# The xbc projection's column tiles emitted one by one between the parts of two other mixers

## The chip, the cores and the metric

The kernel runs on one core of one Trainium2 chip (trn2). The metric is the device time of one execution in microseconds (us); the median over several runs counts. TensorE multiplies matrices into PSUM, ScalarE (ACT) copies PSUM results out and evaluates functions, VectorE (DVE) does elementwise work and scans, GpSimd (POOL) a little elementwise work, and SyncE (SP) issues the DMA transfers between HBM and SBUF.

## The reference, cut to what matters

Two network blocks follow each other on a sequence of 1024 tokens with 1024 features. The second begins with one projection whose columns feed three independent mixers:

```python
proj = h @ w_in                       # 1024 x 1024 tokens by features, times 1024 x 2312
z, xbc, dt_raw, u_s5, x_rg, g_rg = split(proj)   # 512, 1024, 8, 256, 256, 256 columns
xbc = silu(causal_dwconv(xbc, conv_w, conv_b))   # feeds the ssd mixer (8 chunks of 128 tokens)
y_s5 = s5_mixer(u_s5, ...)            # complex linear scan, gelu, a 256 x 256 gate
y_rg = rglru_mixer(x_rg, g_rg, ...)   # conv, two gates, linear scan, times gelu(g_rg)
y = concat([ssd_mixer(z, xbc, dt_raw), y_s5, y_rg]) @ w_out
h = layer_norm(ALPHA * h + y)         # then attention and an MLP
```

The xbc columns are needed only by the ssd mixer. The s5 and rg mixers do not read them.

## The kernel before, in words

The program is written as Python that emits instructions in order. At build time a scheduler fixes the order of each engine's queue: of the instructions whose inputs and buffers it expects to be there, it takes the one that was emitted first, so work emitted later can fill a hole if nothing it needs is missing. On the chip each queue runs strictly in that fixed order. SBUF buffers come from tagged pools with a fixed count of 4 KB-per-partition pages (line 51 and after): 8 of tag X, 8 of W, 8 of H, 6 of S, 3 of bc. Projections write into two PSUM buffers of tag mm.

Activations stand in SBUF as a pair of tiles, high and low part (tag U). A weight column block is loaded by `wcols` (line 100): 256 columns are two pages of 512 KB that are loaded into S (L91), cast to a high part in W by ACT (L82), and the low part is formed in W by DVE (L83); so a block of 256 columns takes 4 of the 8 W pages and, while it is loaded, 2 S pages. `feat_out` (line 367) then multiplies one 128-column tile by one half of the tokens with `mm3`: 8 slices times three matmuls (L114, L115, L116), 24 matmuls into one mm buffer.

The order of emission after the first block is `dt_proj`, `s5_mixer`, `xbc_proj`, `rg_mixer`, `ssd_setup`, the load of the output weights (`wout_load`, L659), then the eight ssd blocks woven with the output stage.

- `s5_mixer` (L1548 and after): a projection of 256 columns, transposes, 64 small matmuls (L1584), a chain on DVE of multiplications, two scans (L1598) and a complex product (L1360 to L1365), then for two halves m: 48 small matmuls each (L1625, L1628), a DVE addition (L1638), transposes (L1644), copies out by ACT (L1646, L1647), a gelu; and last a 256 x 256 gate (L1661 to L1667). It uses ten X pages: two each for UT, U, the scans Are and Aim, and H (eight at once), then one x for each half m.
- `xbc_proj` (L1179): four blocks c of 256 columns, two tiles each, j = 0 to 7. A tile is two `feat_out` calls, for each two ACT instructions that read the PSUM buffer (L1193 into `raw`, L1194 into `o`), then three DVE instructions (L1176), a tanh (L1197), a product (L1198) and the store to the DRAM tensor s_xbc (L1199). `raw` and `o` are X pages.
- `rg_mixer` (L1291): a projection of 256 columns with a conv, the load of the gate columns (Wg), 16 gate matmuls with Sigmoid and Tanh on ACT (L1329 to L1334), functions Ln, Exp and Sqrt on ACT (L1338 to L1343), scans on DVE (L1345), then the projection with Wg whose result is copied to X pages (L1351, L1352), gelu, product, store.
- `ssd_block(i)` loads a slice of all eight xbc tiles (L1213), so it waits for the last tile's store. It takes an S page at L1233 and feeds TensorE at L1243 to L1258.

Of the kernel before, what the change touches and what calls it, by code (L numbers as in the profile page):

```python
# [14 lines left out]
S = 1024  # L15
# [348 lines left out]
class Mix1(Net):  # L364
# [305 lines left out]
    def out_stage(self, W, srcs, res, finish):  # L670

        nc = self.nc
        for i in range(NB):
# [5 lines left out]
            if i == 0:  # L679
                P = self.page_pair()  # L680
            M = [P[z][:, :, 128 * i:128 * i + 128] if i < 4 else
                 self.page("H", F32R).rearrange("p (k c) -> p k c", c=128) for z in range(2)]
            self.split(st, M[0], M[1])
            y = self.page("H")
            nc.sync.dma_start(out=y, in_=_rows(res, i))
            for n in range(2):
                c = slice(512 * n, 512 * n + 512)
                ps = self.ps()
                self.mm3(ps, [(M[0][:, j, :], M[1][:, j, :]) for j in range(8)], W[n])
                self.add_res(y[:, c], ps, True)  # L690
# [371 lines left out]
class Mix2(Mix1):  # L1062


    def kv_mem(self):
        nc, I = self.nc, self.I
        M = [tuple(self.page("X", F32R, [128, 4, 256]) for _ in range(2)) for _ in range(2)]
        for t in range(2):
# [110 lines left out]
    def xbc_proj(self, T):  # L1179
        nc, I = self.nc, self.I  # L1180
        hw = self.small([128, 40], tag="hw", bufs=1)
        nc.vector.tensor_scalar(out=hw[:, 0:32], in0=self.pvec("ssd_conv_w"), scalar1=0.5, scalar2=None, op0=ALU.mult)
        nc.vector.tensor_scalar(out=hw[:, 32:40], in0=self.pvec("ssd_conv_b"), scalar1=0.5, scalar2=None, op0=ALU.mult)
        self.s_xd = self.dram([128, 8, S], "s_xbc")
        for c in range(4):
            W = self.wcols(I["w_in_2"], 512 + 256 * c, 256)
            for m in range(2):
                j = 2 * c + m
                raw, o = self.page("X"), self.page("X")
                for h in range(2):  # L1190
                    sl = slice(512 * h, 512 * h + 512)
                    ps = self.feat_out(T, W, slice(128 * m, 128 * m + 128), h)
                    nc.scalar.copy(out=raw[:, sl], in_=ps)  # L1193
                    nc.scalar.activation(out=o[:, sl], in_=ps, func=ACTF.Identity, scale=hw[:, 4 * j + 3:4 * j + 4],  # L1194
                                         bias=hw[:, 32 + j:33 + j])
                self.conv(o, raw, hw[:, 4 * j:4 * j + 4])
                nc.scalar.activation(out=raw, in_=o, func=ACTF.Tanh)  # L1197
                nc.vector.scalar_tensor_tensor(out=o, in0=raw, scalar=1.0, in1=o, op0=ALU.add, op1=ALU.mult)  # L1198
                nc.sync.dma_start(out=self.s_xd[:, j, :], in_=o)  # L1199

    def ssd_setup(self):
        self.s_St = self.half()
# [88 lines left out]
    def rg_mixer(self, T):  # L1291
        nc, I = self.nc, self.I
        w = I["w_in_2"]
        gw = self.page("H").rearrange("p (z m c) -> p z m c", z=4, c=128)
        nc.vector.memset(gw[:, 0:2], 0.0)
        for z, name in enumerate(("rg_wa_2", "rg_wx_2")):
            for h in range(4):
                r = slice(64 * (h % 2), 64 * (h % 2) + 64)
                nc.sync.dma_start(out=gw[r, z, h // 2, 64 * (h % 2):64 * (h % 2) + 64], in_=I[name][h])
        sm = self.small([128, 8], tag="rgs", bufs=1)  # L1300
        nc.vector.tensor_scalar(out=sm[:, 0:2], in0=self.pvec("rg_lambda"), scalar1=-1.0, scalar2=None, op0=ALU.mult)
        self.softplus(sm[:, 0:2], 2)
        nc.vector.tensor_scalar(out=sm[:, 2:4], in0=sm[:, 0:2], scalar1=8.0, scalar2=None, op0=ALU.mult)
        nc.vector.tensor_scalar(out=sm[:, 0:2], in0=sm[:, 0:2], scalar1=-8.0, scalar2=None, op0=ALU.mult)
        ba = self.pvec("rg_ba")
        nc.vector.tensor_scalar(out=sm[:, 6:8], in0=self.pvec("rg_bx"), scalar1=0.5, scalar2=None, op0=ALU.mult)
        self.rg_od = self.dram([128, 2, S], "rg_od")
        cw, cb = self.pvec("rg_conv_w"), self.pvec("rg_conv_b")
        Wx = self.wcols(w, 1800, 256)
        xcs = []  # L1310
        for m in range(2):
            raw, xc = self.page("X"), self.page("X")
            for h in range(2):
                sl = slice(512 * h, 512 * h + 512)
                ps = self.feat_out(T, Wx, slice(128 * m, 128 * m + 128), h)
                nc.scalar.copy(out=raw[:, sl], in_=ps)
                nc.scalar.activation(out=xc[:, sl], in_=ps, func=ACTF.Identity, scale=cw[:, 4 * m + 3:4 * m + 4],
                                     bias=cb[:, m:m + 1])
            self.conv(xc, raw, cw[:, 4 * m:4 * m + 4])
            xcs.append(xc)  # L1320
        Wg = self.wcols(w, 2056, 256)
        ms = []
        for m in range(2):
            xc = xcs[m]
            r, gx, t = self.page("H"), self.page("H"), self.page("H")
            for h in range(2):
                sl = slice(512 * h, 512 * h + 512)
                ps = self.ps("tr")
                nc.tensor.matmul(out=ps, lhsT=gw[:, 0, m], rhs=xc[:, sl], start=True, stop=True)  # L1329
                nc.scalar.activation(out=r[:, sl], in_=ps, func=ACTF.Sigmoid, bias=ba[:, m:m + 1])  # L1330
                ps = self.ps("tr")
                nc.tensor.matmul(out=ps, lhsT=gw[:, 1, m], rhs=xc[:, sl], start=True, stop=True)
                nc.scalar.activation(out=gx[:, sl], in_=ps, func=ACTF.Tanh, scale=0.5, bias=sm[:, 6 + m:7 + m])
            nc.scalar.activation(out=t, in_=r, func=ACTF.Tanh, scale=sm[:, 2 + m:3 + m])  # L1334
            nc.vector.scalar_tensor_tensor(out=gx, in0=gx, scalar=1.0, in1=xc, op0=ALU.add, op1=ALU.mult)
            ms.append((xc, r, gx, t))
        for m, (xc, r, gx, t) in enumerate(ms):
            nc.scalar.activation(out=xc, in_=t, func=ACTF.Ln, bias=1.0)  # L1338
            nc.scalar.activation(out=xc, in_=xc, func=ACTF.Exp, scale=-1.0)
            nc.scalar.activation(out=r, in_=r, func=ACTF.Exp, scale=sm[:, m:m + 1])  # L1340
            nc.vector.tensor_tensor(out=t, in0=t, in1=xc, op=ALU.mult)
        for m, (xc, r, gx, t) in enumerate(ms):
            nc.scalar.activation(out=t, in_=t, func=ACTF.Sqrt, scale=0.5)  # L1343
            nc.vector.tensor_tensor(out=gx, in0=gx, in1=t, op=ALU.mult)
            nc.vector.tensor_tensor_scan(out=t, data0=r, data1=gx, initial=0.0, op0=ALU.mult, op1=ALU.add)  # L1345
        for m, (xc, r, gx, t) in enumerate(ms):
            x, q = self.page("X"), self.page("X")
            for h in range(2):
                sl = slice(512 * h, 512 * h + 512)
                ps = self.feat_out(T, Wg, slice(128 * m, 128 * m + 128), h)  # L1350
                nc.scalar.activation(out=x[:, sl], in_=ps, func=ACTF.Copy, scale=0.5)  # L1351
                nc.scalar.activation(out=q[:, sl], in_=ps, func=ACTF.Square)  # L1352
            self.gelu(x, q, q)
            nc.vector.tensor_tensor(out=t, in0=t, in1=q, op=ALU.mult)
            nc.sync.dma_start(out=self.rg_od[:, m, :], in_=t)
# [192 lines left out]
    def s5_mixer(self, T):  # L1548
# [19 lines left out]
        for m in range(2):  # L1568
            for q in range(2):
                ps = self.ps("tr")  # L1570
                for j in range(4):
                    g = 4 * q + j
# [30 lines left out]
        a = [v3(x)[:, :, i0] for x in (Are, Aim)]  # L1603
        p = [v3(x)[:, :, i0] for x in (co, sn)]
        self.cmul(v3(H[0])[:, :, i1], v3(H[1])[:, :, i1], a, p, v3(t)[:, :, i1])
        M = [self.page("H") for _ in range(2)]
        for m in range(2):
            for s in range(8):
# [9 lines left out]
        for m in range(2):  # L1618
            ps = self.ps("sc").rearrange("p (r a c) -> p r a c", r=2, c=128)
            for j in range(4):  # L1620
                a = 4 * m + j
                for r in range(2):
                    rs = slice(64 * r, 64 * r + 64)
                    g = 2 * a + r
# [22 lines left out]
                nc.scalar.activation(out=q[:, sl], in_=ps, func=ACTF.Square)  # L1647
            self.gelu(x, q, x)
            Y.append(x)
        gw = self.half([128, 2, 256])  # L1650
        nc.sync.dma_start(out=gw, in_=I["s5_glu_w_2"].rearrange("(k p) e -> p k e", p=128))
        gb = self.small([128, 8], tag="s5t", bufs=20)
# [2 lines left out]
        for m in range(2):  # L1655
            g, o = self.page("H"), self.page("H")
# [126 lines left out]
def build(tc, I, out):  # L1783
    from contextlib import ExitStack
    with ExitStack() as ctx:
        n = Mix2(tc, ctx, I, out)
        n.modulation()
        n.kv_mem()
        def run(g):
            while True:  # L1790
                try:
                    next(g)
                except StopIteration as e:
                    return e.value
# [7 lines left out]
        T, steps = None, [3, 0, 1, 0, 1]  # L1802
        while T is None:
# [4 lines left out]
            T = next(norm)  # L1808
# [11 lines left out]
        T = run(n.block1_out())  # L1820
        T = n.block1_mlp(T)
        n.dt_proj(T)
        n.s5_mixer(T)
        n.xbc_proj(T)
        n.rg_mixer(T)
        n.ssd_setup()
        n.wout = n.wout_load(I["w_out_2"])
        out = n.block2_out()
        T = next(out)
        run(n.weave(n.pipe(n.ssd_block(i) for i in range(NB)), delay(out, 3)))  # L1830
        T = run(n.attention(T))
# [87 lines left out]
```

## Time and profile before

| | us |
|---|---|
| median of 3 runs | 2733.69 (2730.89 to 2739.81) |
| the profiled execution | 2723.2 |
| its span (first to last instruction) | 2721.4 |
| TensorE matmul busy in the span | 2572.5 |

The views give the times from the start of the span. "PEclk" is the share of full TensorE clock that was granted: 1.00 is 2.4 GHz and 0.50 is 1.2 GHz. The engine named with an arrow behind an idle time is what ended that idle time.

### The profile page before, as it was taken

How to read it: one execution, taken by the hardware profiler on the slowest of the kernel's cores; microseconds unless marked ns; L12 is line 12 of the kernel's file. 1: busy time of each engine (PE TensorE's matmuls, PEld its weight loads, DVE VectorE, ACT ScalarE, POOL GpSimd, SP SyncE). 2: the span in 40 equal slices, each digit the busy share in tenths (PEclk: the TensorE clock that was granted, in tenths of full speed). 3: DMA queues.
4: the chain of work that ended last, by engine and by line, in shares of the span. 5: the costliest groups of instructions: out<-in, count | busy, mean ns of one | idle time of the engine just before them, and what ended most of it. 6: DMA issues, size and time to landing. Idle time of an engine off the chain costs nothing.

```text
span 2721.4 us, 32892 instructions
## 1 busy us (share of the span) xinstructions
PE 2572.5 (95%) x12086; PEld 2085.6 (77%) x12086; DVE 1908.2 (70%) x3237; ACT 1113.8 (41%) x1669; POOL 265.8 (10%) x238
## 2 busy tenths in 40 slices
PE   7898999889999999999999997999997999999997
PEld 7576777677888888888876765778876888888885
DVE  5847765788897777555954558785566877767759
ACT  3522233224654444433642462452236444444332
POOL 4112135540000000000000004200000000000000
PEclk8899999999999999999997998999998999999998
DMA  9674423454266669857641313371101756699774
GB/s 332 210 232 142 147 98 102 142 150 147 78 224 217 214 234 324 287 177 240 202 153 47 110 62 105 111 242 40 54 21 73 246 195 224 230 325 333 271 234 145
DMA packets 255130, 484.36 MB, mean 178 GB/s; under 512 B 21604, under 2 KB 110964, under 8 KB 254968
## 3 DMA queue, kind: packets, MB, share of 16 engines
q1 hardware_dynamic: 247768, 470.59, 51.3%
q10 hardware_dynamic: 7200, 11.67, 1.2%
q8 instruction: 95, 1.56, 0.2%
q14 instruction: 67, 0.55, 0.1%
HBM read 338.80 MB, written 143.38 MB: 177 GB/s over the span
## 4 chain that ended last, share of the span: by engine, by line
PE 76%; DVE 10%; DMA 4%; ACT 4%; issue 3%; POOL 2%; SPq 0%; ACTq 0%; DVEq 0%; POOLq 0%
PE ps L114 23%; PE ps L116 23%; PE ps L115 23%; ACT half L186 1%; PE ps L182 1%; DMA H<-r_qk 1%; DVE half L543 1%; POOL X L522 1%; DMA H<-g_qkb 1%; DMA bc<-in_w_ada 1%; DVE st L155 1%; PE ps L1628 1%; DVE W L83 1%; PE ps L535 1%; POOL W L83 0%
## 5 line engine op out<-in xcount | busy, mean ns | idle before, releaser
L114 PE MATMUL ps<-U,W 128*128 128x512 f32 (+1 forms) x1080 | 426.2, 395 | 11.4 <-ACT X L1352 5.9
L83 DVE TENSOR_TENSOR W<-S,W 128x1024 fp32r<-128x1024 f32 (+1 forms) x272 | 332.8, 1225 | 147.9 <-ACT W L82 145.9
L114 PE MATMUL ps<-W,H 128*128 128x512 f32 x1088 | 425.1, 391 | 3.6 <-DVE sm L167 3.0
L115 PE MATMUL ps<-U,W 128*128 128x512 f32 (+1 forms) x1080 | 424.1, 393 | 0.1
L115 PE MATMUL ps<-W,H 128*128 128x512 f32 x1088 | 424.0, 390 | 0.0
L116 PE MATMUL ps<-W,H 128*128 128x512 f32 x1088 | 423.9, 390 | 0.0
L116 PE MATMUL ps<-U,W 128*128 128x512 f32 (+1 forms) x1080 | 423.5, 392 | 0.0
L82 ACT CAST W<-S 128x1024 fp32r<-128x1024 f32 x288 | 299.2, 1043 | 282.0 <-PE ps L115 200.0
L83 DVE TENSOR_TENSOR H<-S,H 128x1024 fp32r<-128x1024 f32 x130 | 158.8, 1222 | 149.3 <-ACT H L82 138.5
L82 ACT CAST H<-S 128x1024 fp32r<-128x1024 f32 x130 | 136.5, 1050 | 288.6 <-PE ps L115 211.9
L114 PEld LDWEIGHTS ps<-U,W 128*128 128x128 f32 (+1 forms) x1080 | 201.1, 186 | 59.9 <-ACT X L1352 6.3
L114 PEld LDWEIGHTS ps<-W,H 128*128 128x128 f32 x1088 | 204.6, 188 | 47.7 <-DVE X L1014 3.7
L115 PEld LDWEIGHTS ps<-U,W 128*128 128x128 f32 (+1 forms) x1080 | 201.1, 186 | 47.0 <-DVE U L336 2.5
L116 PEld LDWEIGHTS ps<-W,H 128*128 128x128 f32 x1088 | 204.4, 188 | 42.2 <-DVE H L83 0.2
L115 PEld LDWEIGHTS ps<-W,H 128*128 128x128 f32 x1088 | 204.6, 188 | 41.9
L116 PEld LDWEIGHTS ps<-U,W 128*128 128x128 f32 (+1 forms) x1080 | 200.7, 186 | 45.0 <-issue 0.7
L114 PE MATMUL ps<-W,U 128*128 128x512 f32 x352 | 142.0, 403 | 0.0
L115 PE MATMUL ps<-W,U 128*128 128x512 f32 x352 | 140.6, 399 | 0.2 <-DVE W L83 0.2
L116 PE MATMUL ps<-W,U 128*128 128x512 f32 x352 | 140.4, 399 | 0.1
L767 ACT ACTIVATE ev<-ev 128x512 f32<-128x512 f32 x104 | 65.5, 630 | 138.8 <-DVE ev L865 117.3
L1239 POOL TENSOR_TENSOR half<-tri,s_adt 128x512 f32<-128x512 f32 x16 | 19.6, 1233 | 884.5 <-DVE half L1116 778.2
L768 ACT ACTIVATE X<-ev 128x512 f32<-128x512 f32 x128 | 81.1, 636 | 3.5
(527 smaller groups left out, 4606.5 us busy)
## 6 DMA issues: line engine op xcount, KB each, us to landing
S<-mlp_h SPq DMA_DIRECT2D x112, 512.0 KB, 4.8
S<-in_w_ff SPq DMA_DIRECT2D x96, 512.0 KB, 5.1
mlp_h<-X SPq DMA_DIRECT2D x96, 512.0 KB, 3.9
S<-in_mlp_w SPq DMA_DIRECT2D x96, 512.0 KB, 5.2
mlp_w<-S SPq DMA_DIRECT2D x96, 256.0 KB, 2.8
S<-mlp_w SPq DMA_DIRECT2D x48, 512.0 KB, 4.8
S<-in_w_in SPq DMA_DIRECT2D x46, 512.0 KB, 5.2
bc<-in_w_ada SPq DMA_DIRECT2D x32, 512.0 KB, 5.0
```

The source lines that it names most:

```text
L82: self.nc.scalar.copy(out=hi, in_=src)
L83: (lo_eng or self.nc.vector).tensor_tensor(out=lo, in0=src, in1=hi.bitcast(F32), op=ALU.subtract)
L114: mm(out=ps, lhsT=lh, rhs=rh, start=start and k == 0, stop=False)
L115: mm(out=ps, lhsT=lh, rhs=rl, start=False, stop=False)
L116: mm(out=ps, lhsT=ll, rhs=rh, start=False, stop=stop and k == n - 1)
L155: self.nc.vector.bn_stats(out=st[:, h, :], in_=y[:, h * 512:(h + 1) * 512])
L182: nc.tensor.transpose(ps[:, j * 128:(j + 1) * 128], y[:, k * 128:(k + 1) * 128], self.ident)
L186: nc.scalar.activation(out=full[:, j * 128:(j + 1) * 128], in_=ps[:, j * 128:(j + 1) * 128], func=ACTF.Identity, scale=scale[:, k:k + 1], ...
L522: nc.gpsimd.tensor_tensor(out=E[:, l, :].rearrange("p (g c) -> p g c", c=2 * w), in0=bv, in1=bv[:, :, w - 1:w].broadcast_to([128, 64 // w, ...
L535: nc.tensor.matmul(out=ps[:, r, u, :], lhsT=k[rs] if l < 0 else E[rs, l, :], rhs=q[rs] if l < 0 else qt[rs, l, :], start=True, stop=True)
L767: nc.scalar.activation(out=r, in_=x, func=ACTF.Relu)
L768: nc.scalar.activation(out=out, in_=r, func=ACTF.Square)
```

## The change

`xbc_proj`, `s5_mixer` and `rg_mixer` become generators that pause at the marked places, and the driver takes 3 tiles of xbc after the first part of s5, 1 after its second part, 1 after the rg projection, 3 after the rg gates. The third pause of `rg_mixer` takes none, since all eight tiles are out by then. The pages of a tile change their tags: `raw` from X to S, `o` from X to bc. No instruction is added or removed.

```diff
             for m in range(2):
                 j = 2 * c + m
-                raw, o = self.page("X"), self.page("X")
+                raw, o = self.page("S"), self.page("bc")
...
                 nc.sync.dma_start(out=self.s_xd[:, j, :], in_=o)
+                yield
...
             self.conv(xc, raw, cw[:, 4 * m:4 * m + 4])
             xcs.append(xc)
+        yield
         Wg = self.wcols(w, 2056, 256)
...
             ms.append((xc, r, gx, t))
+        yield
         for m, (xc, r, gx, t) in enumerate(ms):
             nc.scalar.activation(out=xc, in_=t, func=ACTF.Ln, bias=1.0)
...
             nc.vector.tensor_tensor_scan(out=t, data0=r, data1=gx, initial=0.0, op0=ALU.mult, op1=ALU.add)
+        yield
         for m, (xc, r, gx, t) in enumerate(ms):
             x, q = self.page("X"), self.page("X")
...
         self.cmul(v3(H[0])[:, :, i1], v3(H[1])[:, :, i1], a, p, v3(t)[:, :, i1])
+        yield
         M = [self.page("H") for _ in range(2)]
...
             Y.append(x)
+        yield
         gw = self.half([128, 2, 256])
...
-        n.s5_mixer(T)
-        n.xbc_proj(T)
-        n.rg_mixer(T)
+        xbc = n.xbc_proj(T)
+        for g, side in ((n.s5_mixer(T), (3, 1)), (n.rg_mixer(T), (1, 3))):
+            for _ in g:
+                for _ in range(side[0] if side else 0):
+                    next(xbc, None)
+                side = side[1:]
+        run(xbc)
```

## Rows read from the trace of the kernel before

**Rows 1.** The page's first part: busy time, share of the span, instructions

```profile
PE 2572.5 (95%) x12086; PEld 2085.6 (77%) x12086; DVE 1908.2 (70%) x3237; ACT 1113.8 (41%) x1669; POOL 265.8 (10%) x238
```

**Rows 2.** Busy time by stretch (window, length, PE, PEld, DVE, ACT, POOL, PEclk, DMA share, GB/s)

```profile
1449.70:1456.40 6.70, 1.23 (x5) 0.92 (x4) 6.60 (x6) 0.00 (x0) 0.00 (x0) 0.72 0.00 0
1456.40:1490.20 33.80, 32.54 (x107) 24.76 (x108) 6.83 (x8) 4.75 (x9) 0.00 (x0) 0.50 0.00 0
1502.40:1596.60 94.20, 94.20 (x417) 77.97 (x417) 51.89 (x42) 40.57 (x54) 0.66 (x1) 1.00 0.28 102
1596.60:1617.90 21.30, 21.28 (x82) 13.97 (x80) 7.77 (x7) 20.32 (x23) 0.00 (x0) 1.00 0.25 75
1617.90:1623.90 6.00, 0.10 (x2) 0.01 (x1) 4.61 (x5) 5.97 (x8) 0.00 (x0) 0.95 0.00 0
1623.90:1636.30 12.40, 12.40 (x49) 10.08 (x50) 12.37 (x12) 9.01 (x13) 0.67 (x1) 0.89 0.23 72
1636.30:1686.90 50.60, 35.82 (x157) 25.36 (x155) 45.26 (x68) 14.25 (x27) 30.36 (x20) 0.76 0.37 111
```

**Rows 3.** Timeline of PE: start, us, engine, line, op, tiles [idle before <- releaser]

```profile
1455.16 1.22 PE L1628 MATMUL ps<-H,X 64*128 64x128 f32 x4 [5.44 <-DVE X L1362]
```

**Rows 4.** Timeline of DVE: first and last instruction of the s5 chain, 15 rows

```profile
1438.48 1.23 DVE L1591 TENSOR_TENSOR X<-ps,H 128x1024 f32<-128x1024 f32 x1 [5.09 <-PE ps L1584]
...
1456.39 1.22 DVE L1365 TENSOR_TENSOR X<-X,H 128x1016 f32<-128x1016 f32 x1
```

**Rows 5.** Timeline of ACT: the copies of the s5 halves and the first of xbc

```profile
1476.39 0.60 ACT L1646 ACTIVATE X<-ps 128x512 f32<-128x512 f32 x1 [39.23 <-PE ps L1644]
...
1489.17 0.60 ACT L1646 ACTIVATE X<-ps 128x512 f32<-128x512 f32 x1 [0.26 <-PE ps L1644]
...
1491.10 0.62 ACT L1193 COPY X<-ps 128x512 f32<-128x512 f32 x1
```

**Rows 6.** Waits of SP, 1440 to 1640: total us, times, longest

```profile
SPq L1667 <- ACT H L1665: 58.9, 2, 57.9
```

**Rows 7.** Tile X, 1400 to 1640: duration ns min/median/max, first and last start

```profile
L1176 DVE SCALAR_TENSOR_TENSOR X<-X,hw,X x24: 1279/1283/1286, 1493.6 to 1579.9; 128x1023 f32<-128x1023 f32 x8, 128x1022 f32<-128x1022 f32 x8, 128x1021 f32<-128x1021 f32 x8
...
L1193 ACT COPY X<-ps x16: 567/588/655, 1491.1 to 1576.0; 128x512 f32<-128x512 f32 x16
L1194 ACT ACTIVATE X<-ps,hw x16: 760/784/841, 1491.6 to 1576.4; 128x512 f32<-128x512 f32 x16
L1197 ACT ACTIVATE X<-X x8: 1047/1061/1062, 1498.9 to 1581.3; 128x1024 f32<-128x1024 f32 x8
L1198 DVE SCALAR_TENSOR_TENSOR X<-X,X x8: 1220/1226/1228, 1500.2 to 1582.4; 128x1024 f32<-128x1024 f32 x8
```

**Rows 8.** DMA issues in three windows: count, KB each, median us to landing

```profile
S<-in_w_in SPq DMA_DIRECT2D x3, 512.0 KB, 4.2
...
s_xbc<-X SPq DMA_DIRECT2D x3, 512.0 KB, 2.6
...
H<-s_xbc SPq DMA_DIRECT2D x4, 512.0 KB, 4.3
```

**Rows 9.** Timeline: one cast and one low part of a weight page

```profile
1509.72 1.05 ACT L82 CAST W<-S 128x1024 fp32r<-128x1024 f32 x1 [0.76 <-PE ps L115]
...
1510.80 1.23 DVE L83 TENSOR_TENSOR W<-S,W 128x1024 fp32r<-128x1024 f32 x1 [0.59 <-ACT W L82]
```

**Rows 10.** Timeline: a table load of ACT, and the held-up gate projection on PE

```profile
1619.57 1.28 ACT L1343 ACT_TABLE_LOAD   x1
...
1623.89 0.79 PE L114 MATMUL ps<-U,W 128*128 128x512 f32 x1 [5.90 <-ACT X L1352]
```

**Rows 11.** Timeline: SP's first ssd load, POOL's first S page, PE's first output matmul

```profile
1599.62 27.53 SPq L1213 DMA_DIRECT2D H<-s_xbc  x2
...
1635.63 1.96 POOL L1233 TENSOR_TENSOR S<-H,s_dt 128x512 f32<-128x512 f32 x1 [132.58 <-DVE X L83]
...
1686.93 0.48 PE L114 MATMUL ps<-W,U 128*128 128x512 f32 x1
```

## The prediction

> **What bounds the kernel now.** I read the page's busy shares first. TensorE carries matmuls in 95% of the span [rows 1], so the time can fall only where TensorE is idle or runs at the lower of its two clock levels. I then cut the stretch between the s5 projection and the output stage into windows [rows 2], and looked up who released TensorE in each hole.
>
> Two holes stand there. The first begins at 1449.7: in 6.7 us TensorE is busy 1.23, and afterwards, from 1456.4 to 1490.2, it is busy all the time but at PEclk 0.50, which is 1.2 GHz. It was released by DVE [rows 3], at the end of the s5 chain, which occupies DVE alone from 1438.48 to 1457.6 [rows 4]. The second hole is 1617.9 to 1623.9, busy 0.10 of 6.0; the gate projection waits there 5.90 us for ACT's L1352 [rows 10], because ACT is busy 20.32 of the 21.3 us before with the rg functions. Between the two, from 1502.4 to 1596.6, TensorE is busy throughout at PEclk 1.00 while ACT is busy 40.57 and DVE 51.89 of 94.2 us [rows 2]. So the xbc stretch has spare ACT and DVE time, and the s5 and rg stretches lack TensorE work.
>
> Why did xbc not fill the first hole by itself? ACT has nothing to do for 39.23 us before 1476.39, yet the first `raw` is written at 1491.10, right behind the copies of the second s5 half at 1489.17 [rows 5]. The scan pages Are and Aim are X pages too and were last read when the chain ended at 1457.6 [rows 4], so two X pages were free for over 30 us. I read this as: pages of one tag are given out in the order of emission, and `raw` stood behind both x pages of s5. Without `raw`, the two mm buffers stay full and TensorE can do only the first tile.
>
> **The change part by part.**
>
> *The size of a tile.* 417 matmuls in 94.2 us [rows 2] are 0.226 us each, so a tile of 48 takes 10.8 us, and a projection of 96 takes 21.7 us.
>
> *First hole.* With S and bc pages, tiles 0 and 1 are free to run while DVE does the s5 chain: 10.8 us each from about 1440, so until about 1461.6, beyond the chain's end at 1457.6. The idle time of 5.5 us in the first window and 1.3 us in the second goes: 6.7 us. And TensorE comes into the s5 matmuls at the upper level. These 32.54 us at 0.50 [rows 2] would take 16.3 at 1.00; not all of it need scale with the clock, so the bounds are 0 and 16.3. I take 15, close to the upper one, since the stretch shows no idle time beside the clock.
>
> *Second hole.* The Ln, Exp, Sqrt and scan work between the rg gates and the gate projection gets three tiles, 32.4 us of TensorE work, beside it, where before it had the gate projection alone. The 5.9 us go, and so does 11% of the next 12.4 us at PEclk 0.89 [rows 2], 1.4 us. Together the recoverable time is 6.7 + 15 + 5.9 + 1.4 = 29.0 us. The xbc matmuls themselves are only moved.
>
> *What is new: when weights are loaded.* `raw` now stands in S between the weight loads. By the order of emission the block c = 1 can be loaded only when tile 1's `raw` has its page, the rg columns after tile 3's, Wg after tile 4's, c = 3 after tile 5's. From there a page needs 4.2 us to land [rows 8], a cast of 1.05 and a low part of 1.23 [rows 9], 6.5 us, while the second half of the tile gives 5.4 us of cover. So each boundary can cost between 0 and 6.5 us. For c = 1 the s5 matmuls stand ready; for the rg columns the s5 gate does; Wg is not needed until the end: I take 0 for these. For c = 3 the cover is thinnest: Wg keeps four of the eight W pages, so its cast must wait for the end of tile 5, and then 1.05 and 1.23 us pass: I take 2.5 us.
>
> *Queues.* On SP the eight xbc stores and the later weight loads now stand before and between the s5 and rg transfers. SP was free for this: it waited 57.9 us in one piece on the s5 store [rows 6]. A store that waits for its product holds up the weight load behind it; tile j's product comes 0.59 + 0.78 + 3 x 1.28 + 1.06 + 1.23 = 7.5 us after its last matmul [rows 7], later than the next `raw` at 5.4 us, so the load is ahead of it and I take 0, with the 6.5 us above as the upper bound. POOL's queue gets nothing new.
>
> *ACT and DVE.* A tile takes ACT 2 x (0.59 + 0.78) + 1.06 = 3.8 us and DVE 3 x 1.28 + 1.23 = 5.1 us [rows 7], both under its 10.8 us. The tanh of tiles 5 to 7 falls between functions of rg that need other tables; at most two further loads of 1.28 us [rows 10] for each, 7.7 us of ACT. From the rg projection to tile 7 TensorE has at least 21.7 + 4 x 10.8 = 65 us. ACT has the rg stretch's own 20.32 + 5.97 = 26.3 us, its loads included [rows 2], the added loads 7.7, copies of the projection 5.5, four tiles 15 and six casts 6.3: 61 us. That fits, so I take 0; the cover is thin, and if each added load holds TensorE up, 7.7 us come back.
>
> The Trainium skill, "ScalarE: Activation LUTs", section "Table sets: the hidden batching unit", speaks against this: functions of one table set should be batched together. Its section "What ACT_TABLE_LOAD costs" puts a switch at about 2.66 us with the drain. By that page the twelve loads would be an estimated 16.6 us dearer, ACT would need 77 us beside 65, and 12 us of the sum would be lost. The load's row shows 1.28 us and nothing behind it, so the sum goes by the row.
>
> *What is late next.* The last tile. Tile 7 ends one gate projection, 21.7 us, before the end of that projection, which moves from 1636.3 to about 1636.3 - 29.0 + 2.5 = 1610, so tile 7 ends at 1588. Its product is there 7.5 us later, the store lands in 2.6 and the ssd slice in 4.3 [rows 8], so it is in SBUF at 1602.4 and the time of two issues. POOL's first S page, before at 1635.63 behind the casts of the output weights [rows 11], hangs on the gate projection and moves to about 1610, so the slice is just in time; its transposes and copies may lie 2 us behind. Bounds: 8 us better (DVE, busy 45.26 of the last 50.6 us, has done its scans earlier) to 20 us worse (rival below). I take 2 us.
>
> *The sum.* 29.0 - 2.5 - 2.0 = 24.5 us. The profiled execution took 2723.2 us, span 2721.4 and 1.8 around it, so 2698.7. The median of the runs shown stands 10.5 us above this execution; on that scale 2733.7 - 24.5 = **2709.2 us**.
>
> **The rivals.**
>
> *The s5 matmuls stay at 1.2 GHz.* For it: small matmuls run at 0.50 for 33.8 us without a hole, and PEclk averages 0.76 in the ssd stretch, which is made of such matmuls. Against: xbc matmuls, which run at 1.00 for 94.2 us, would stand directly before them and between the halves. Then 15 us are missing: gain 9.5, 2724.
>
> *ACT becomes the bound of the rg stretch.* For it: it is at 95% there already [rows 2], and its queue is strictly in order. Against: it is at 43% in the xbc stretch that the rg functions would share. If each of the six added loads holds TensorE up, 7.7 us come back: 2717. By the skill's switch cost it would be 12 us and 2721; the load row does not bear that out.
>
> *The last tile sets the pace.* From the slice's issue at 1599.62 to the first output matmul at 1686.93 lie 87 us [rows 11]. If that is one chain, it starts at 1598 instead and only about 5 us remain: 2728. Against: most of it waits on other things, among them POOL's S page.
>
> *The change does not do what it says.* If S or bc pages are not there when tile 0 wants them (the weight loads of later blocks fill S), the first hole stays and only 7.3 - 2.5 us remain: 2729.
>
> *Slower: weights arrive late at every block.* The place is SP's queue: a store that waits for its product stands ahead of each load. Then five boundaries (c = 1, rg, c = 2, Wg, c = 3) cost the whole 6.5 us, 32.5, and holes that long bring the lower clock as the first one did, some 1.4 us each as after the second hole, 7 more. 2733.7 - 29 + 39.5 = 2744. It decides against the change where a boundary costs over 29 / 5 = 5.8 us.
>
> **How the numbers follow.** About 0.3%, 8.2 us, is what a measurement of this kernel can tell from no change. Chances: forecast 0.60, s5 slow 0.10, ACT 0.09, last tile 0.08, not done 0.06, slower 0.07. The forecast, s5 slow and ACT are faster by over 8.2 us: 0.79. Last tile and not done are within it: 0.14. Slower: 0.07. The range reaches down to the forecast with its open terms at their better bounds (1.3 for the clock, 2.5 for c = 3, 10 for the ssd start: 13.8 less, 2695) and up to the rival at 2728, leaving out what lies above.
>
> **What would show it.** Right: no hole of TensorE between 1440 and 1490 and PEclk 1.00 on the s5 matmuls; `raw` of tile 0 written at about 1446; the gate projection without the wait on L1352, ending at about 1610; SP's longest wait far under 57.9 us; a gap of 2 to 3 us before tile 6. Wrong: PEclk 0.50 on L1625 and L1628; idle time of TensorE before a first matmul of a block, released by DVE's L83 or ACT's L82; the ssd stretch longer than 50.6 us by what was gained before it.

## The result, and the profile after

| | before | after |
|---|---|---|
| median, us | 2732.29 (2730.53 to 2739.81, 4 runs) | 2697.55 (2695.02 to 2704.22, 4 runs) |
| ratio | | 0.9871, 95% interval 0.9845 to 0.9898 |
| the profiled execution, us | 2723.2 | 2696.28 |
| its span, us | 2721.4 | 2694.4 |

The changed kernel is faster by 35 us by the medians and by 26.9 us between the two profiled executions. The forecast was 2709.2 in a range of 2695 to 2728. Why the two differences are not the same is told with the steps below; the trace first.

The page's first part of the kernel after (busy us, share of the span, instructions), against [rows 1]:

```profile
PE 2557.3 (95%) x12086; PEld 2074.0 (77%) x12086; DVE 1899.9 (71%) x3237; ACT 1114.3 (41%) x1671; POOL 262.2 (10%) x238
```

The same 12086 matmuls take 15.2 us less of TensorE. Outside of them the span had 2721.4 - 2572.5 = 148.9 us before and has 2694.4 - 2557.3 = 137.1 now, 11.8 less. So of the 27.0 us of the span a little more lies in shorter matmuls than in idle time.

To leave out what happens ahead of the change, times below are also given from an anchor: the start of the 64 small matmuls from which the DVE chain of s5 sets out (L1584 before, L1588 after), at 1436.47 before and 1433.49 after. The two stretches behind it, up to the last matmul of the gate projection and from there to the first of the output stage, in the kernel before (columns as in [rows 2]); the third row is the stretch of s5's small matmuls, L1625 and L1628:

```profile
1436.47:1636.03 199.56, 186.92 (x798) 145.36 (x797) 109.68 (x95) 90.70 (x118) 6.04 (x5) 0.90 0.22 71
1636.03:1686.93 50.90, 36.12 (x159) 25.57 (x157) 45.56 (x68) 14.52 (x27) 30.66 (x20) 0.77 0.38 112
1455.16:1486.27 31.11, 29.82 (x101) 23.02 (x101) 5.62 (x6) 3.12 (x5) 0.00 (x0) 0.50 0.00 0
```

And in the kernel after: the same two stretches, three windows of 20 us in which the tiles now run, and the stretch of the s5 matmuls (from 1474.43):

```profile
1433.49:1606.35 172.86, 169.56 (x782) 130.59 (x782) 109.29 (x94) 93.33 (x118) 6.01 (x4) 1.00 0.32 103
1606.35:1659.37 53.02, 39.29 (x176) 29.05 (x175) 44.63 (x71) 17.52 (x33) 27.47 (x20) 0.81 0.37 107
1440.00:1460.00 20.00, 18.84 (x83) 15.05 (x81) 19.94 (x18) 6.99 (x11) 0.00 (x0) 1.00 0.00 0
1460.00:1480.00 20.00, 19.68 (x91) 15.53 (x91) 11.37 (x10) 5.44 (x7) 0.00 (x0) 1.00 0.43 131
1474.43:1492.54 18.11, 18.11 (x107) 13.98 (x106) 6.29 (x7) 4.18 (x6) 0.00 (x0) 1.00 0.45 145
1560.00:1580.00 20.00, 18.62 (x79) 14.78 (x80) 14.56 (x12) 19.86 (x23) 0.00 (x0) 1.00 0.31 103
```

The first row of each block: 26.7 us shorter. PEclk is 1.00 where it was 0.90 in the mean, and the time outside of matmuls went from 12.6 to 3.3 us. The second row got 2.1 us longer, but its idle time did not: 50.90 - 36.12 = 14.8 before, 53.02 - 39.29 = 13.7 after. It has 17 more matmuls, and the first has 16 fewer: these moved behind the boundary. So the two belong together: 250.46 us before, 225.88 after, **24.6 us gained**, of it 14.2 in the busy time of almost as many matmuls (957 and 958 by these rows) and 10.4 in idle time. From the anchor to the end of the span it is 2721.4 - 1436.47 = 1284.9 against 2694.4 - 1433.49 = 1260.9, so 24.0; what lies behind the first output matmul takes 0.6 longer.

The holes of TensorE that are left, from its timeline (start, us, line, tiles, idle time before and releaser), with the first of the s5 matmuls, which answers to [rows 3], and the first output matmul, which answers to [rows 11]:

```profile
1433.49 3.71 PE L1588 MATMUL ps<-X,H 128*64 128x128 f32 x64
...
1458.85 0.50 PE L114 MATMUL ps<-U,W 128*128 128x512 f32 x1 [1.00 <-ACT W L82]
1460.32 0.51 PE L116 MATMUL ps<-U,W 128*128 128x512 f32 x1 [0.47 <-DVE W L83]
...
1474.43 0.71 PE L1633 MATMUL ps<-H,X 64*128 64x128 f32 x4
...
1561.03 0.50 PE L114 MATMUL ps<-U,W 128*128 128x512 f32 x1 [1.12 <-ACT W L82]
1562.55 0.50 PE L116 MATMUL ps<-U,W 128*128 128x512 f32 x1 [0.32 <-DVE W L83]
...
1595.57 0.50 PE L114 MATMUL ps<-U,W 128*128 128x512 f32 x1 [0.19 <-ACT X L1356]
...
1621.00 2.07 PE L1244 MATMUL ps<-half,tri 128*128 128x512 f32 x2 [4.83 <-POOL half L1240]
...
1659.37 0.47 PE L114 MATMUL ps<-W,U 128*128 128x512 f32 x1
```

The 5.44 us before the s5 matmuls are gone, since tile 0 and the following ones stand there. The 5.90 us of the gate projection [rows 10] have become 0.19 (L1356 is the L1352 of before). New are two boundaries between weight blocks, c = 1 with 1.00 + 0.47 = 1.47 us and c = 3 with 1.12 + 0.32 = 1.44. The largest hole is now the one behind POOL at the start of the ssd blocks.

ACT's first copy of tile 0, which answers to the L1193 of [rows 5], and SP's longest waits from 1440 to 1640 (total, times, longest), which answer to [rows 6]:

```profile
1441.57 0.59 ACT L1193 COPY S<-ps 128x512 f32<-128x512 f32 x1 [7.38 <-PE ps L116]
```

```profile
SPq L1199 <- DVE bc L1198: 110.5, 8, 27.4
SPq L1673 <- ACT H L1671: 28.4, 2, 27.4
```

Tile 0's `raw` is written 8 us after the anchor, before it was 54.6. SP waits for eight products in turn, 110.5 us in all, and yet no hole of TensorE up to the end of the gate projection is put down to a transfer: the two at the block boundaries are released by ACT's casts and DVE's low parts.

### The profile page after: what moved, and what is told of

The parts are those of the page before. It is cut to its first block, busy times and chain, and to the rows that moved or that the text cites. A ratio compares the mean times of both kernels' runs of the same rounds, so it can differ in the third digit from the quotient of the medians.

```text
span 2694.4 us, 32855 instructions
## 1 busy us (share of the span) xinstructions
PE 2557.3 (95%) x12086; PEld 2074.0 (77%) x12086; DVE 1899.9 (71%) x3237; ACT 1114.3 (41%) x1671; POOL 262.2 (10%) x238
## 4 chain that ended last, share of the span: by engine, by line
PE 75%; DVE 10%; DMA 4%; ACT 4%; issue 3%; POOL 3%; SPq 0%; POOLq 0%; ACTq 0%; DVEq 0%
PE ps L114 23%; PE ps L116 23%; PE ps L115 23%; DMA H<-r_qk 1%; DVE half L543 1%; PE ps L182 1%; ACT half L186 1%; POOL X L522 1%; DMA H<-g_qkb 1%; DMA bc<-in_w_ada 1%; DVE st L155 1%; DMA S<-in_xa_wk 1%; DVE W L83 1%; PE ps L535 0%; DVE bc L1176 0%
## 5 line engine op out<-in xcount | busy, mean ns | idle before, releaser
L83 DVE TENSOR_TENSOR W<-S,W 128x1024 fp32r<-128x1024 f32 (+1 forms) x272 | 330.4, 1217 | 116.6 <-ACT W L82 116.2
L82 ACT CAST W<-S 128x1024 fp32r<-128x1024 f32 x288 | 298.8, 1043 | 259.0 <-PE ps L115 176.7
L83 DVE TENSOR_TENSOR H<-S,H 128x1024 fp32r<-128x1024 f32 x130 | 159.2, 1225 | 151.0 <-ACT H L82 146.3
L82 ACT CAST H<-S 128x1024 fp32r<-128x1024 f32 x130 | 136.6, 1051 | 291.7 <-PE ps L115 223.8
L1240 POOL TENSOR_TENSOR half<-tri,s_adt 128x512 f32<-128x512 f32 x16 | 20.1, 1268 | 892.3 <-DVE half L1118 778.2
```

What stands on the lines that cost most here:

```text
L82: self.nc.scalar.copy(out=hi, in_=src)
L83: (lo_eng or self.nc.vector).tensor_tensor(out=lo, in0=src, in1=hi.bitcast(F32), op=ALU.subtract)
```

## The experiments

The theories. (1) **Pages**: tile 0 of xbc could not fill the first hole because its pages are X pages, which it gets behind the x pages of s5; other tags alone undo that. The rival: the order of emission does it, and the tags only make room. (2) **Clock**: the s5 matmuls run at the level that TensorE brings into them. The rival: they pull the clock down themselves, or it falls by chance in an execution. (3) **rg**: the second hole goes because xbc tiles stand beside the rg functions, which only the order can bring. (4) The 13.7 us idle before the output stage: are they the price of the change, or was the stage like that?

One table for all runs. "Timed" is the median against that of before on the same chip; the ratio beside it is taken over all timed runs and not from the two medians. The other columns are of the profiled execution, us from the anchor: the start of the last matmul of the gate projection, the first output matmul, the end of the span, and the gain of the last against 1284.9. There is one profile of each kernel, and two of before and of the whole change: the latter two differ by 1.6, 1.8 and 0.4 us in the three columns. How many matmuls stand ahead of the first output matmul also differs (957 in the whole change, 939 with only the rg pauses, 928 with the rg tail later), so versions are compared by the end of the span.

| run | timed / before | ratio, 95% interval | gate end | first output | span end | gain |
|---|---|---|---|---|---|---|
| before | | | 199.6 | 250.5 | 1284.9 | |
| before again | 2723.64 (1 run) | | 199.4 | 250.4 | 1284.9 | 0.0 |
| after | 2697.55 / 2732.29 | 0.9871, 0.9845 to 0.9898 | 172.9 | 225.9 | 1260.9 | 24.0 |
| after again | 2698.98 / 2728.72 | 0.9895, 0.9869 to 0.9921 | 174.5 | 224.1 | 1261.3 | 23.6 |
| tags alone | 2702.36 / 2728.48 | 0.9907, 0.9887 to 0.9926 | 182.0 | 229.1 | 1264.4 | 20.5 |
| order alone | 2712.38 / 2728.48 | 0.9941, 0.9918 to 0.9963 | 184.9 | 237.2 | 1273.5 | 11.4 |
| only the s5 pauses | 2704.35 / 2728.48 | 0.9915, 0.9894 to 0.9936 | 181.6 | 231.5 | 1267.9 | 17.0 |
| only the rg pauses | 2699.79 / 2728.48 | 0.9895, 0.9875 to 0.9915 | 173.5 | 217.4 | 1258.5 | 26.4 |
| spare matmuls | 2709.52 / 2728.72 | 0.9944, 0.9917 to 0.9970 | 187.0 | 234.7 | 1269.8 | 15.2 |
| rg tail later | 2702.06 / 2728.72 | 0.9909, 0.9882 to 0.9936 | 193.1 | 219.3 | 1264.7 | 20.2 |
| the same, s5 unpaused | 2704.92 / 2728.72 | 0.9921, 0.9893 to 0.9950 | 192.9 | 219.0 | 1265.6 | 19.3 |
| rg tail in other pages | 2704.99 / 2721.96 | 0.9932, 0.9918 to 0.9947 | 172.8 | 229.9 | 1262.8 | 22.1 |

**Tags alone.** The kernel before, with the new tags and nothing else:

```diff
-                raw, o = self.page("X"), self.page("X")
+                raw, o = self.page("S"), self.page("bc")
```

> Only the tags of the xbc pages change (raw in S, o in bc); the order of emission stays s5, xbc, rg. Theory A (the pages were what held xbc out of the first hole, and the planner fills a hole with later work by itself): the first hole closes without any interleaving, the s5 matmuls run at PEclk 1.00, the time falls by about 20 us (6.7 idle and 13 to 15 of the lower clock), and the second hole with its 5.9 us wait on ACT's L1352 stays. Theory B (the interleaved order is what counts): no gain, within 5 us of before.

Measured: 26.1 us under the kernel before. The stretch of its s5 matmuls (columns as in [rows 2]), and then its longest wait of TensorE from the anchor to the end of the gate projection (total, times, longest):

```profile
1460.32:1476.87 16.55, 16.55 (x102) 13.04 (x101) 9.69 (x9) 5.96 (x9) 0.00 (x0) 1.00 0.37 128
```

```profile
PE ps L114 <- ACT X L1352: 5.9, 1, 5.9
```

The s5 matmuls take 16.55 us at PEclk 1.00 where they took 31.11 at 0.50, and the second hole stands untouched with its 5.9 us. So the scheduler put the tiles into the first hole of its own accord, as soon as their pages were there: the page theory holds, and the first hole with its clock is most of the whole change (20.5 of 24.0 us from the anchor).

**Order alone.** The whole change with the pages of before:

```diff
-                raw, o = self.page("S"), self.page("bc")
+                raw, o = self.page("X"), self.page("X")
```

> Only the order of emission changes as in the change; raw and o stay X pages. Theory A: the first hole stays, since the first raw needs an X page and none is free before the s5 chain has ended at about 1457; the s5 matmuls still begin at PEclk 0.50; three tiles then share the few free X pages and hold up s5; the rg hole closes: gain between 0 and 8 us, or a loss. Theory B: the gain of the whole change, about 25 us or more.

Measured: 16.1 us under before, 10 us behind tags alone. TensorE still waits in the first hole, now for the copies of tile 0, and then the clock does something of interest. Its windows around the hole, and the stretch of its s5 matmuls; then the waits of TensorE, and ACT's first copy of tile 0:

```profile
1450.00:1455.00 5.00, 2.60 (x13) 2.01 (x11) 5.00 (x5) 0.00 (x0) 0.00 (x0) 0.99 0.00 0
1455.00:1460.00 5.00, 0.00 (x0) 0.00 (x0) 4.90 (x5) 1.58 (x3) 0.00 (x0) 0.50 0.00 0
1460.00:1465.00 5.00, 4.68 (x11) 3.71 (x12) 4.56 (x4) 0.95 (x3) 0.00 (x0) 0.50 0.00 0
1465.00:1470.00 5.00, 5.00 (x23) 4.06 (x23) 1.23 (x1) 1.64 (x2) 0.00 (x0) 0.99 0.36 121
1484.56:1502.00 17.44, 17.44 (x104) 13.64 (x103) 8.19 (x8) 6.21 (x9) 0.00 (x0) 1.00 0.07 30
```

```profile
PE ps L114 <- ACT X L1194: 12.4, 2, 7.7
```

```profile
1455.91 1.07 ACT L1193 COPY X<-ps 128x512 f32<-128x512 f32 x2 [15.64 <-DVE X L1368]
```

Within the hole of 7.7 us the clock fell to 0.50, and the kernel before leaves its hole at 0.50 too. But xbc matmuls came first behind it, and in the second window of 5 us behind it the level was back at 0.99, so the s5 matmuls ran at 1.00 in spite of the hole. The page theory was right on the hole and wrong on the clock: it had expected the s5 matmuls at 0.50 here, and a gain of 0 to 8 us; the other theory had expected 25 or more. Order by itself has a value, that of what stands behind the hole. The second hole is not there in its old form, but 4.7 us of waiting for tile copies stand at 1589.36.

The ACT row also parts two things that the page theory ran together. Here `raw` is emitted ahead of the x pages of s5, and still it is written only 16.3 us after the anchor, when DVE's complex product releases the first X page, and `o` follows at 19.9; before, `raw` was written at 54.6. So until the hole was nearly over, the two X pages of a tile were not free, whatever the order; the order of emission explains the 38 us behind it.

**Only the s5 pauses**, the rest of xbc out before rg begins; and **only the rg pauses**, with s5 run through and four tiles after it:

```diff
-        for g, side in ((n.s5_mixer(T), (3, 1)), (n.rg_mixer(T), (1, 3))):
+        for g, side in ((n.s5_mixer(T), (3, 1)), (xbc, ()), (n.rg_mixer(T), ())):
```

> New tags, four tiles between the s5 parts, the other four before rg, nothing between the rg parts. Theory A: first hole closed, second hole open: about the time of the tags alone, 6 to 9 us above the whole change. Theory B (the interleaving with rg brings nothing): the time of the whole change within 3 us.

```diff
-        for g, side in ((n.s5_mixer(T), (3, 1)), (n.rg_mixer(T), (1, 3))):
+        run(n.s5_mixer(T))
+        for _ in range(4):
+            next(xbc)
+        for g, side in ((n.rg_mixer(T), (1, 3)),):
```

> New tags, s5 emitted in one piece, then four tiles, then rg with one and three tiles between its parts. Theory A (tags alone close the first hole): within 3 us of the whole change, so that pauses in s5 are not needed. Theory B (tiles must be emitted ahead of the later s5 parts to be taken): first hole open, 15 to 22 us above the whole change.

Measured: 24.1 and 28.7 us under before. The first is not to be told from tags alone and keeps the wait of 5.9 us (first fence, waits of TensorE). By its ratio the second is not to be told from the whole change, and it has only the boundary of c = 3 and 0.2 us at the gate projection left, beside a wait of 1.6 us in the s5 halves that tags alone has too (second fence, the same view):

```profile
PE ps L114 <- ACT X L1356: 5.9, 1, 5.9
...
PE ps L114 <- ACT W L82: 1.0, 1, 1.0
```

```profile
PE ps L1649 <- DVE H L1643: 1.6, 1, 1.6
PE ps L114 <- ACT W L82: 1.2, 1, 1.2
PE ps L116 <- DVE W L83: 0.3, 1, 0.3
PE ps L114 <- ACT X L1356: 0.2, 1, 0.2
```

So the pauses in s5 add nothing to the tags, and those in rg are what takes the second hole away. The four kernels with new tags part the two, by the gain from the anchor: neither pause 20.5, only s5 17.0, only rg 26.4, both 24.0 and 23.6. The rg pauses are worth 5.9 without and 6.6 to 7.0 with the s5 pauses (by the medians on one chip less, 2.6 without them). The s5 pauses cost 2.4 to 3.5 in these profiles, but the two kernels with the later rg tail below differ by 0.9 the other way, and the medians do not settle it.

**Spare matmuls.** The kernel before, and 32 matmuls whose result nobody reads; the scheduler puts them between the 64 small matmuls and tile 0, so that tile 0 still runs where the hole was. It adds work to the computation and takes none away:

```diff
+        ps = self.ps("tr")
+        for k in range(32):
+            nc.tensor.matmul(out=ps, lhsT=T[0][0][:, k % 8, 0:128], rhs=T[0][0][:, k % 8, :], start=True, stop=True)
```

> The kernel before with 32 spare matmuls, 7.2 us, whose result nobody reads, put by the planner between the 64 small s5 matmuls and the first xbc tile; nothing else is changed. Theory A (the larger part of the first hole is the clock: dense matmuls up to the end of the s5 chain keep it at 2.4 GHz): the s5 matmuls run at PEclk 1.00 in 16 to 18 us instead of 31, and the time falls by 10 to 15 us although 7 us of useless work were added. Theory B (the s5 matmuls are slow by themselves, or fall to 1.2 GHz for lack of activity): no gain, or 1 us slower.

Measured: 19.2 us **faster** than before by the medians (about 15 by the ratio, 15.2 from the anchor), with 7.6 us of useless work in the program. These matmuls in the timeline of TensorE (start, us), and the stretch of its s5 matmuls:

```profile
1438.69 7.56 PE L1608 MATMUL ps<-U 128*128 128x512 f32 x32
```

```profile
1455.51:1472.35 16.84, 16.82 (x102) 13.12 (x101) 3.88 (x5) 3.12 (x5) 0.00 (x0) 1.00 0.00 1
```

The s5 matmuls start 20.5 us after the anchor (18.7 before), so nothing was won ahead of them; they end 37.3 after it, before it was 49.8. No SBUF page and no order of the tiles was changed, so what remains is the level of the clock that TensorE had when it came in. The clock theory is shown, and that the small matmuls pull the level down is excluded: they kept 1.00 for 16.8 us.

**After again**, an unchanged copy of the whole change, on the chip of spare matmuls and of the next two:

> The whole change, unaltered, beside the others on one chip. Theory A: 2695 to 2701 us, about 3 to 6 us under the tags alone and within 3 us of the version with tiles between the rg parts only. Theory B (the pauses in s5 matter as well): clearly under both.

Measured: 29.7 us under before, and 23.6 us from the anchor, against 24.0. The profile repeats; the difference of the medians does not to the same degree, 34.7 and 29.7.

**The rg tail later.** If it is the rg tail that holds ACT and DVE up when the ssd blocks start, weave its gate projection into them, in two kernels, the second with s5 unpaused as well:

```diff
-            x, q = self.page("X"), self.page("X")
+            x, q = self.page("bc"), self.page("S")
...
             nc.sync.dma_start(out=self.rg_od[:, m, :], in_=t)
+            yield
...
-        run(n.weave(n.pipe(n.ssd_block(i) for i in range(NB)), delay(out, 3)))
+        def late():
+            yield from rg
+            yield from delay(out, 1)
+        run(n.weave(n.pipe(n.ssd_block(i) for i in range(NB)), late()))
```

> The whole change, and the rg gate projection (two halves of 10.8 us) is emitted woven with the first ssd blocks instead of before them, with its x in bc and q in S so that the output weights need not wait for it. Theory A (what is left is the ssd start, 53 us with 13.7 us idle and PEclk 0.81, for lack of matmuls that do not depend on the last tile): the wait on POOL's L1240 and the lower clock there shrink, 5 to 12 us faster than the whole change. Theory B (the ssd start is a chain on DVE and POOL that other matmuls cannot shorten, and moved work ends later): within 3 us, or slower.

> As the one before, with s5 emitted in one piece and four tiles after it (no pauses in s5). Theory A (pauses in s5 are not needed once the tags are changed): within 3 us of the one before. Theory B: 5 us or more slower than it.

Measured: 3 and 6 us slower than the whole change on the same chip, so theory B of the first holds and nothing is saved; the two differ by 2.9 us, just within the 3 of the second's theory A. The wait of TensorE at the start of the ssd stretch, of the first of them:

```profile
PE ps L1220 <- DMA H<-s_xbc: 8.8, 1, 8.8
```

The second shows 10.0 at the same place. The gate projection was the cover for the last tile's store and the load of its slice; taken away, TensorE waits for them. Here the mechanism of the last tile, one of the rivals, can be seen at work; in the change itself the cover holds. The first output matmul does come 5 us sooner (219.3 and 219.0 against 224.1), with some 30 fewer matmuls ahead of it, and the span ends 3 to 4 us later; where that is lost is open.

**The rg tail in other pages.** The first half of the gate projection (m = 0) keeps its place; the second is emitted behind the load of the output weights and the first part of the ssd blocks. So this kernel changes two things at once:

```diff
-            x, q = self.page("X"), self.page("X")
+            x, q = self.page("bc"), self.page("S")
...
             nc.sync.dma_start(out=self.rg_od[:, m, :], in_=t)
+            yield
...
         run(xbc)
+        next(rg)
...
-        run(n.weave(n.pipe(n.ssd_block(i) for i in range(NB)), delay(out, 3)))
+        def late():
+            yield from rg
+            yield from delay(out, 2)
+        run(n.weave(n.pipe(n.ssd_block(i) for i in range(NB)), late()))
```

> The whole change, and the last pages of rg (x, q of its gate projection) from bc and S instead of X, so that rg's tail needs no X page and the output weights' casts on ACT are not queued behind it; the last pause of rg is taken before the ssd set-up. Theory A (the 13.7 us idle at the start of the ssd stretch come from ACT and DVE being taken up by rg's tail until then): the first output-stage matmul comes 2 to 6 us sooner than 225 us after the anchor, and the kernel is 2 to 6 us faster than the whole change. Theory B (that idle time comes from POOL and the first slice's work, which the tail does not hold up): the first output matmul stays within 2 us of 225 and the time within 3 us of the whole change.

Measured: 17.0 us under before of its chip, and the first output matmul at 229.9 from the anchor, not sooner than 225 and not within 2 us of it but 4 to 6 later, so both theories missed. TensorE's longest waits at the start of the ssd stretch:

```profile
PE ps L1220 <- DMA H<-s_xbc: 4.9, 1, 4.9
PE ps L1252 <- DVE half L1262: 4.9, 2, 2.8
PE ps L1244 <- POOL half L1240: 4.4, 2, 3.6
```

The first of them can be followed in SP's queue:

```profile
1601.48 0.32 SPq L1199 DMA_DIRECT2D s_xbc<-bc  x1
1601.89 7.42 SPq L659 DMA_DIRECT2D S<-in_w_out  x6
1612.35 0.34 SPq L1359 DMA_DIRECT2D rg_od<-H  x1
1612.80 0.37 SPq L659 DMA_DIRECT2D S<-in_w_out  x1
1613.22 6.50 SPq L1214 DMA_DIRECT2D H<-s_xbc  x4
```

The first slice (L1214) stands behind a run of six loads of the output weights and one more, and is issued 172.3 us after the anchor; in the whole change all eight of these loads are out by 1597.14, and the slice is issued at 166.1 (1599.62). Whether the pages or the place of the second half put the loads there, one kernel with both cannot tell; it shows only that the two together bring the ssd start nothing. So the theory that rg's tail delays the ssd start found no support and is not refuted for the pages by themselves. The idle time before the output stage is no price of the change, since the stretch had 14.8 us of it before and has 13.7 now; what sets it is not settled beyond the row of POOL's L1240 above. Whether this kernel is slower than the whole change was not measured on one chip.

**Before again**, one more profile of the unchanged kernel:

> The kernel before, unchanged, profiled once more: is its s5 stretch the same in each execution? Theory A (hole and clock belong to the program): the 64 small s5 matmuls start near 19 us after the stage's anchor, take 31 us at PEclk 0.50, and the gate projection's last matmul comes 199 to 200 us after the anchor, all within 1 us of the first profile. Theory B (the clock's fall is a matter of the single execution, and part of the scatter of this kernel's times comes from it): the small matmuls take 17 to 30 us, or the last gate matmul moves by over 3 us.

The stretch of its s5 matmuls:

```profile
1455.68:1486.80 31.12, 29.84 (x101) 23.03 (x101) 5.62 (x6) 3.12 (x5) 0.00 (x0) 0.50 0.00 0
```

31.12 us at 0.50, 199.4 us to the gate's end, 1284.9 to the end of the span: the same to 0.2 us. In two profiles of two the hole and the clock are there: they belong to the program.

## Why the prediction was right

The sign, the sum and the main mechanism were right: two holes filled with tiles, and the s5 matmuls at the upper level. By its steps:

- **The sum**, 24.5 us: 24.6 at the first output matmul, 24.0 at the end of the span. That it fits to a tenth is luck, for two errors cancel: clock 16.4 predicted (15 + 1.4), 14.2 measured; idle time 8.1 predicted (6.7 + 5.9 - 2.5 - 2), 10.4 measured.
- **First hole and clock.** The 6.7 us of idle time went. The clock was worth less than 15: in tags alone the busy time of the s5 stretch fell from 29.82 to 16.55, 13.3 us; the window of 32.54 us that was used held other matmuls too. By itself the first hole gave 17 to 20.5 us (only the s5 pauses, tags alone), where 21.7 stood.
- **The reading of the pages.** That X pages kept tile 0 out is shown by tags alone. That it was the order of emission is half of it: order alone shows that the two X pages of a tile came free only towards the end of the hole. Tile 0's `raw` came 4.4 us sooner than the 1446 forecast, of which 3.0 lie ahead of the anchor.
- **Second hole.** The 5.90 us became 0.19.
- **Weights.** c = 3 cost 1.44 us, not 2.5. c = 1, taken at 0, cost 1.47; the rg columns, c = 2 and Wg show no hole (the 0.19 is a wait for a copy of the gate projection). Together 2.9 against 2.5, and PEclk in the windows of both boundaries stayed at 1.00. These two holes are what the prediction named as a sign of being wrong, idle time before a block's first matmul released by L82 or L83; it came, but small. The upper bound of 6.5 us was far too high. SP's timeline and ACT's show why:

```profile
1430.92 0.78 SPq L1614 DMA_DIRECT2D H<-s_K  x2
1431.74 0.98 SPq L91 DMA_DIRECT2D S<-in_w_in  x2
```

```profile
1456.81 1.06 ACT L1197 ACTIVATE S<-bc 128x1024 f32<-128x1024 f32 x1 [3.10 <-DVE bc L1176]
1457.77 1.02 ACT L82 CAST W<-S 128x1024 fp32r<-128x1024 f32 x1
```

  The two loads for c = 1 are issued at 1431.74, before tile 0 has even begun to be read out at 1441.57, while the prediction let them wait for tile 1's `raw`. The order of the pages did not make this load late. The cast came late for another reason, which the prediction does not have: it stands in ACT's queue right behind tile 0's tanh, and that waited 3.10 us for DVE, which does tile 0's conv between the parts of the s5 chain. The s5 matmuls that were to cover this boundary still waited for the same chain.
- **ACT.** Up to six table loads more were counted; the trace has nine in the rg stretch where it had seven, so two more. ACT is 19.86 of 20 us busy from 1560 to 1580, and no hole of TensorE there but that of c = 3 is put down to it. No load takes more than its 1.28 us, with the function at once behind it:

```profile
1560.99 1.28 ACT L1342 ACT_TABLE_LOAD   x1
1562.29 1.06 ACT L1342 ACTIVATE X<-X 128x1024 f32<-128x1024 f32 x1
```

  The Trainium skill, "ScalarE: Activation LUTs", section "What ACT_TABLE_LOAD costs", gives about 1.28 us for the load and with a drain about 2.66 us for a switch, by which the prediction estimated a loss of 12 us; this trace agrees with the load and shows no drain beside it.
- **The ssd start.** 2 us longer was forecast and 2.1 came, but for another reason: 17 matmuls moved into the stretch, while its idle time fell by 1.1. The first slice is issued at 1599.62:

```profile
1599.62 0.56 SPq L1214 DMA_DIRECT2D H<-s_xbc  x1
```

  The first output matmul comes 59.8 us later, not 87: the rival of the last tile is refuted. (Its price did not follow from its terms either: a chain that starts at 1598 instead of 1599.62 leaves 1.6 us and not about 5.) The step that failed is the 2 us put down to slice and copies.
- **From the profile to the median.** The weakest step. The profile was forecast at 2698.7 and came at 2696.28; the 2.4 us are less than the 3.0 that lie ahead of the anchor, where the order of the work is nearly the same. The 10.5 us between the profiled execution of before and its median were carried over as if they belonged to any version; after has its profiled execution 1.3 us under its median. That is 9.2 us of the 11.7 by which 2709.2 is too high. None of the open terms for which the range had room is of this kind, so that the median still fell into the range is luck. The timed runs of before on four occasions lie between 2711.6 and 2739.8, those of after between 2694.7 and 2704.2, and the two profiles of before agree from the anchor on. What the runs do show is that the time goes with the mean granted clock: before has 0.969 at 2711.58 us and 0.959 at 2736.07 on one chip, 0.965 at 2721.07 and 0.956 at 2737.63 on another, and the whole change 0.970 to 0.973 in all its ten runs. In which stretch the timed runs of before lose their clock is open, since only the profiled executions left a trace.

Of the rivals, "s5 stays at 1.2 GHz" is refuted by spare matmuls and by PEclk 1.00; "ACT", "last tile" and "slower" by the rows above and the measured time; "does not do what it says" by tile 0's `raw`.

## What to carry to other kernels

When an engine idles while independent work stands ready, look up which buffer that work takes first, whether any is free at that time, and who stands ahead of it in the order of emission: here one line of tags gave most of what the whole change gave. Of a hole of TensorE count the clock behind it as well, and look at what stands behind it: here small matmuls took 31.1 us instead of 16.6, while matmuls of 512 columns brought the level back. A median that stands apart from the profiled execution is not an offset to be carried to the next version.

## What was not expected of the hardware

The clock's level, once at 1.2 GHz, stayed there under the small s5 matmuls: in the kernel before TensorE was busy without a hole from 1460 to 1485, at PEclk 0.50 in each of five windows of 5 us. The same level under xbc matmuls, in order alone, rose from 0.50 to 0.99 from one window of 5 us to the next. And the same small matmuls that did not bring it back did not lose it either: entered at 1.00 they kept 1.00 for 16.8 us. So 32 matmuls of no use, 7.6 us long, made a kernel faster by 15.2 us from the anchor (19.2 by the medians, ratio 0.9944).

A second thing is the scatter ahead of the anchor: with an instruction order that is the same up to there, it stands at 1433.3 in one execution (after again) and at 1440.9 in another (the rg tail in other pages), more than some of the differences that were looked for. The two profiles of one kernel lie within 0.5 us of each other there, so whether the execution, the chip or the program makes the scatter is open. Times from an anchor can order versions otherwise than whole spans: only the rg pauses has a longer span than the whole change, 2697.3 against 2694.4, and is 2.4 us shorter from the anchor.
